# The low part of every second weight tile by a negated copy and an adding transfer

## The chip, the cores and the metric

The kernel runs on one core of a Trainium2 chip. The metric is the device time of one execution in microseconds. A profiled execution has besides its time a span, from its first to its last instruction, and every event in it is dated from the start of that span.

## The reference

A trunk of two layers works on 256 latent and 256 context tokens of width 1024. Each layer is a half-step SwiGLU feed-forward, a token mixer (chunked spatial gating beside a bidirectional gated linear recurrence, with one input and one output projection), and a second feed-forward. Cut to what matters here:

```python
def _swiglu(h, w1, w3, w2):
    return (jax.nn.silu(h @ w1) * (h @ w3)) @ w2
...
    for l in range(DEPTH):
        last = l == DEPTH - 1
        ml = _modulation(c, w_ada[l], b_ada[l])
        mc = _modulation(c_ctx[None], w_ada[l], b_ada[l])
        ...
        lat = lat + 0.5 * ml[2] * _swiglu(_modulate(lat, norm_ffn1_g[l], ml[0], ml[1]), *ffn1)
        cx = cx + 0.5 * mc[2] * _swiglu(_modulate(cx, norm_ffn1_g[l], mc[0], mc[1]), *ffn1)
        ...
        lat = lat + ml[5] * out_lat
        ...
        lat = lat + 0.5 * ml[8] * _swiglu(_modulate(lat, norm_ffn2_g[l], ml[6], ml[7]), *ffn2)
        if not last:
            cx = cx + 0.5 * mc[8] * _swiglu(_modulate(cx, norm_ffn2_g[l], mc[6], mc[7]), *ffn2)
    return _rmsnorm(lat, norm_final_g)
```

All weights are float32. In the last layer the context tokens are dropped after the mixer has read them, so the last feed-forward and most of the last mixer work on the 256 latent tokens alone. The modulation vectors (shift, scale, gate) come from `silu(c) @ w_ada`.

## The kernel before, in words

**Three products for one.** TensorE multiplies in the float32r format, which keeps fewer bits than float32. So every operand is held as a high part (the value rounded to float32r) and a low part (the value minus its high part), and `mm3` (L284 to L288) issues three matmuls for each product: high with high, high with low, low with high.

**Weight tiles.** The weights are cut into 362 tiles of up to 4 x 128 rows and 256 columns (512 KB; the last of each six in a down projection has 2 x 128 rows, 256 KB). `plan` (L102) lists them in the order in which they are used. A tile goes through three stages, and `pump` (L156) drives them:

- load: SyncE issues a transfer into a `wraw` buffer (L172 to L174). There are N_RAW = 3 of them, so the load of tile n+3 reuses the buffer of tile n and is issued right behind the split of tile n in the program.
- split: ScalarE writes the high part `whi` (L187, a copy with rounding), then VectorE writes the low part `wlo` (L191, source minus high part). There are N_SPLIT = 4 pairs of buffers, so the split of tile n waits until TensorE is done with tile n-4. `n_split` counts the splits and so numbers the tiles.
- use: `fm` (L290) and `tm_unit` (L680) run the matmuls of a tile; `done` (L209) counts it as finished.

`take` (L193) hands out the next tile and calls `pump` first, so that the split of tile i+3 is issued when tile i is taken. The same function `split` (L186) makes the parts of the gated activations (`g_hi`, `g_lo`) and of mixer activations (`h_hi`, `h_lo`).

**Modulation loads.** Between weight tiles the plan has 256 ada pieces. SyncE loads each (L166) into one of three `wada` buffers, on the same in-order queue as the weight loads; VectorE adds them up (`acc`, L247 and L249), TensorE turns the sum (`ada_ps`, L258), ScalarE copies it (L261).

**Order.** The schedule is manual: each engine runs its instructions in the order in which the program issues them, and semaphores hold them where data or buffers aren't ready. A feed-forward first runs 11 pairs of 256 hidden columns (two tiles of w1, two of w3 each: 44 tiles) and after each half the gate: silu on ScalarE (L422), the product on VectorE (L424), the split of the result. Then come four down projections of 256 columns, six tiles each. With both token groups a matmul has 512 moving columns; the last quarter of the down projection is done for latent and for context tokens apart (256 columns each, its six tiles loaded twice). In the last feed-forward all matmuls have 256 columns. Four PSUM banks take the products, two at a time.

**GpSimd** has little to do: the constants of the start, and the power in `rstd` (L331) for each norm, which VectorE's `spread` (L356) waits for. No transfer is issued on its queue.

Of the kernel before, what the change touches and what calls it, by code (L numbers as in the profile page):

```python
# [10 lines left out]
F32 = mybir.dt.float32  # L11
F32R = mybir.dt.float32r
U8 = mybir.dt.uint8
AF = mybir.ActivationFunctionType
ALU = mybir.AluOpType
# [57 lines left out]
class Trunk:  # L73
# [82 lines left out]
    def pump(self):  # L156
        nc = self.nc
        moved = True
        while moved:
            moved = False  # L160
            if self.n_load >= 4 and self.a_load < min(len(self.adas), self.a_done + self.N_ADA):
                it = self.adas[self.a_load]
                _, l, j, half, k = it.key
                c0 = j * D + 512 * half
                it.raw = self.wp.tile([P, 512], F32, tag="ada", name="wada", bufs=self.N_ADA)
                nc.sync.dma_start(it.raw, self.io["w_ada"][l, k * P:(k + 1) * P, c0:c0 + 512])  # L166
                self.a_load += 1
                moved = True
            if self.n_load < min(self.cap_load, len(self.ws), self.n_split + self.N_RAW):
                it = self.ws[self.n_load]  # L170
                _, name, l, k0, nk, c0 = it.key
                it.raw = self.wp.tile([P, 4, 256], F32, tag="raw", name="wraw", bufs=self.N_RAW)  # L172
                src = self.io[name][l, k0 * P:(k0 + nk) * P, c0:c0 + 256]
                nc.sync.dma_start(it.raw[:, :nk, :], src.rearrange("(k p) c -> p k c", p=P))  # L174
                self.n_load += 1
                moved = True
            if self.n_split < min(self.cap_split, self.n_load, self.n_done + self.N_SPLIT):
                it = self.ws[self.n_split]
                nk = it.key[4]
                it.hi = self.wp.tile([P, 4, 256], F32R, tag="hi", name="whi", bufs=self.N_SPLIT)  # L180
                it.lo = self.wp.tile([P, 4, 256], F32R, tag="lo", name="wlo", bufs=self.N_SPLIT)
                self.split(it.hi[:, :nk, :], it.lo[:, :nk, :], it.raw[:, :nk, :])
                self.n_split += 1
                moved = True

    def split(self, hi, lo, src):  # L186
        self.nc.scalar.activation(hi, src, AF.Copy)  # L187
        self.low(hi, lo, src)

    def low(self, hi, lo, src):  # L190
        self.nc.vector.tensor_tensor(lo, src, hi.bitcast(F32), op=ALU.subtract)  # L191
# [887 lines left out]
```

## Time and profile before

| what | value |
|---|---|
| time, median of two runs | 1818.21 us (1817.19 and 1819.23) |
| the profiled execution's own time | 1819.16 us |
| its span | 1817.5 us |
| granted TensorE clock, mean | 0.995 |
| bytes moved by transfers | 266.99 MB, 147 GB/s over the span |

In the profile an engine's busy time counts its instructions, not its waits. PE is TensorE's matmuls, PEld its weight loads, DVE VectorE, ACT ScalarE, POOL GpSimd, SP SyncE; a q behind a name means the engine's instruction queue, such as SPq for transfers issued by SyncE. A row of a group reads: line, engine, operation, written tile <- read tiles, shapes, count, then busy microseconds and mean nanoseconds of one, then the idle time just before them and what ended it. Rows of a timeline begin with the start and the duration in microseconds. Matmuls overlap, so the duration of one is longer than the distance between two.

### The profile page before, as it was taken

The page shows a single profiled execution, that of the slowest core. Times are in us where ns is not written, and L with a number is a line of the kernel's source. Part 1 is how long each engine was busy: PE and PEld are TensorE (multiplying, and loading weights), DVE is VectorE, ACT ScalarE, POOL GpSimd, SP SyncE. Part 2 cuts the span into 40 slices and gives each one's busy share as a digit, 9 for nine tenths or more (in the row PEclk, how much of TensorE's full clock was granted, in tenths as well). Part 3 has the DMA queues.
Part 4 walks back from the last instruction along what each step waited for, and adds up shares of the span by engine and source line. Part 5 has one row for each costly group of instructions (what it writes and reads, how often), then busy time and mean ns, then how long its engine had stood idle before and what let it go on. Part 6 is the DMA issues. An engine that isn't in the chain of part 4 may idle for free. (4 is left out here: it accounts for less than half of the span.)

```text
span 1817.5 us, 27049 instructions
## 1 busy us (share of the span) xinstructions
PE 1785.7 (98%) x10853; PEld 1547.7 (85%) x10853; DVE 1125.8 (62%) x1746; ACT 670.5 (37%) x1087; POOL 20.6 (1%) x27
## 2 busy tenths in 40 slices
PE   7999999999999999999999999999999999989998
PEld 5777778899898898777788897777788999979998
DVE  4766676675737666666666676545445767665554
ACT  3322222236444343222222242222222555544443
POOL 0000000000000000000000000000000000000000
PEclk9999999999999999999999999999999999989999
DMA  9555555554212124555454544544454532446653
GB/s 327 167 171 157 173 157 164 181 190 126 70 59 82 59 59 146 153 154 156 145 151 153 185 138 147 159 152 149 153 166 140 157 105 86 136 128 186 186 186 117
DMA packets 230645, 266.99 MB, mean 147 GB/s; under 512 B 10368, under 2 KB 192248, under 8 KB 230520
## 3 DMA queue, kind: packets, MB, share of 16 engines
q1 hardware_dynamic: 230520, 265.27, 47.2%
q8 instruction: 85, 1.39, 0.3%
q14 instruction: 40, 0.33, 0.1%
HBM read 264.18 MB, written 1.05 MB: 146 GB/s over the span
## 5 line engine op out<-in xcount | busy, mean ns | idle before, releaser
L286 PE MATMUL mm<-h_hi,whi 128*128 128x512 f32 (+1 forms) x2016 | 712.2, 353 | 4.9 <-ACT h_hi L383 3.0
L287 PE MATMUL mm<-h_lo,whi 128*128 128x512 f32 (+1 forms) x2016 | 705.2, 350 | 1.5 <-DVE h_lo L372 1.0
L288 PE MATMUL mm<-h_hi,wlo 128*128 128x512 f32 (+1 forms) x2016 | 702.6, 349 | 0.0
L191 DVE TENSOR_TENSOR wlo<-wraw,whi 128x1024 fp32r<-128x1024 f32 x362 | 430.7, 1195 | 371.8 <-ACT whi L187 367.8
L187 ACT ACTIVATE whi<-wraw 128x1024 fp32r<-128x1024 f32 x362 | 370.9, 1031 | 409.0 <-PE mm L287 288.0
L286 PEld LDWEIGHTS mm<-h_hi,whi 128*128 128x128 f32 x2016 | 381.0, 189 | 63.0 <-issue 4.0
L287 PEld LDWEIGHTS mm<-h_lo,whi 128*128 128x128 f32 x2016 | 382.7, 190 | 56.7 <-DVE h_lo L372 5.6
L288 PEld LDWEIGHTS mm<-h_hi,wlo 128*128 128x128 f32 x2016 | 380.7, 189 | 53.5
L286 PE MATMUL mm<-g_hi,whi 128*128 128x256 f32 (+1 forms) x836 | 282.1, 337 | 0.0
L288 PE MATMUL mm<-g_hi,wlo 128*128 128x256 f32 (+1 forms) x836 | 278.8, 334 | 0.0
L287 PE MATMUL mm<-g_lo,whi 128*128 128x256 f32 (+1 forms) x836 | 278.8, 333 | 0.0
L249 DVE SCALAR_TENSOR_TENSOR acc<-wada,cond,acc 128x512 f32<-128x512 f32 x392 | 274.0, 746 | 4.3 <-DMA wada<-in_w_ada_dram 3.4
L286 PEld LDWEIGHTS mm<-g_hi,whi 128*128 128x128 f32 x836 | 158.1, 189 | 18.3 <-issue 2.4
L288 PEld LDWEIGHTS mm<-g_hi,wlo 128*128 128x128 f32 x836 | 158.1, 189 | 16.0
L287 PEld LDWEIGHTS mm<-g_lo,whi 128*128 128x128 f32 x836 | 158.2, 189 | 15.2
L187 ACT ACTIVATE g_hi<-silu 128x512 fp32r<-128x512 f32 (+1 forms) x92 | 51.7, 562 | 182.9 <-DVE silu L424 181.0
L422 ACT ACTIVATE silu<-mm 128x512 f32<-128x512 f32 (+1 forms) x92 | 48.3, 528 | 139.7 <-PE mm L288 135.4
L191 DVE TENSOR_TENSOR g_lo<-silu,g_hi 128x512 fp32r<-128x512 f32 (+1 forms) x92 | 55.7, 605 | 57.9 <-ACT g_hi L187 57.9
L424 DVE TENSOR_TENSOR silu<-silu,mm 128x512 f32<-128x512 f32 (+1 forms) x92 | 54.9, 597 | 36.4 <-PE mm L288 36.4
L286 PE MATMUL mm<-whi,h_hi 128*128 128x256 f32 x224 | 64.3, 287 | 0.0
L287 PE MATMUL mm<-wlo,h_hi 128*128 128x256 f32 x224 | 62.6, 279 | 0.0
L288 PE MATMUL mm<-whi,h_lo 128*128 128x256 f32 x224 | 62.5, 279 | 0.0
(129 smaller groups left out, 1053.0 us busy)
## 6 DMA issues: line engine op xcount, KB each, us to landing
wraw<-in_ffn_w_dram SPq DMA_DIRECT2D x271, 512.0 KB, 4.3
wada<-in_w_ada_dram SPq DMA_DIRECT2D x256, 256.0 KB, 3.2
wraw<-in_w_in_dram SPq DMA_DIRECT2D x56, 512.0 KB, 3.6
a<-in_w_ada_dram SPq DMA_DIRECT2D x8, 1024.0 KB, 9.6
wraw<-in_w_out_dram SPq DMA_DIRECT2D x16, 512.0 KB, 3.9
wraw<-in_ffn_w_dram SPq DMA_DIRECT2D x19, 256.0 KB
x<-in_x_dram SPq DMA_DIRECT2D x2, 512.0 KB
ctx<-in_ctx_dram SPq DMA_DIRECT2D x2, 512.0 KB, 5.8
```

Source lines behind the costliest of these rows:

```text
L187: self.nc.scalar.activation(hi, src, AF.Copy)
L191: self.nc.vector.tensor_tensor(lo, src, hi.bitcast(F32), op=ALU.subtract)
L249: nc.vector.scalar_tensor_tensor(acc[:, s], raw, c, acc[:, s], op0=ALU.mult, op1=ALU.add)
L286: mm(ps, lhsT=l_hi, rhs=r_hi, start=start, stop=False)
L287: mm(ps, lhsT=l_hi, rhs=r_lo, start=False, stop=False)
L288: mm(ps, lhsT=l_lo, rhs=r_hi, start=False, stop=stop)
L422: nc.scalar.activation(silu[j], ps, AF.Silu)
L424: nc.vector.tensor_tensor(silu[j], silu[j], ps, op=ALU.mult)
```

## The change

In `pump`, the odd tiles from number 9 on take another way through the split. ScalarE writes the high part as before, then writes the negated high part (a copy of the source with scale -1 and the same rounding) into the low buffer. A transfer issued on GpSimd's queue then adds the source, from the raw buffer, onto the low buffer, which gives source minus high part. VectorE's subtraction falls away for these tiles. Activations are split as before.

```diff
                 it.lo = self.wp.tile([P, 4, 256], F32R, tag="lo", name="wlo", bufs=self.N_SPLIT)
-                self.split(it.hi[:, :nk, :], it.lo[:, :nk, :], it.raw[:, :nk, :])
+                parts = it.hi[:, :nk, :], it.lo[:, :nk, :], it.raw[:, :nk, :]
+                if self.n_split % 2 and self.n_split > 8:
+                    self.split_by_dma(*parts)
+                else:
+                    self.split(*parts)
                 self.n_split += 1
                 moved = True
...
+    def split_by_dma(self, hi, lo, src):
+
+        nc = self.nc
+        nc.scalar.activation(hi, src, AF.Copy)
+        nc.scalar.activation(lo, src, AF.Copy, scale=-1.0)
+        nc.gpsimd.dma_start(lo.bitcast(F32), src, accum_op=ALU.add)
```

## The prediction

> **What bounds the kernel now.** I read the page first: how full each engine is, and where over the span.
>
> ```profile
> span 1817.5 us, 27049 instructions
> PE 1785.7 (98%) x10853; PEld 1547.7 (85%) x10853; DVE 1125.8 (62%) x1746; ACT 670.5 (37%) x1087; POOL 20.6 (1%) x27
> PE   7999999999999999999999999999999999989998
> DMA  9555555554212124555454544544454532446653
> ```
>
> TensorE is busy for 1785.7 of 1817.5 us in nearly every slice, so all that could be won by feeding it better is 31.8 us, 1.7% of the span. VectorE at 62% and ScalarE at 37% are not the bound. The transfer engines are half busy, and they are busiest in the last eighth; I come back to that. Next the two rows of the split itself, and who waits for it.
>
> ```profile
> L191 DVE TENSOR_TENSOR wlo<-wraw,whi 128x1024 fp32r<-128x1024 f32 x362 | 430.7, 1195 | 371.8 <-ACT whi L187 367.8 <-PE aux L524 2.0 <-PE mm L287 1.3
> L187 ACT ACTIVATE whi<-wraw 128x1024 fp32r<-128x1024 f32 x362 | 370.9, 1031 | 409.0 <-PE mm L287 288.0 <-issue 109.8 <-DMA wraw<-in_ffn_w_dram 4.2
> ```
>
> ```profile
> SPq L174 <- DVE wlo L191: 931.3, 303, 17.1
> ```
>
> The split of a weight tile starts when TensorE gives a whi/wlo buffer back (the 288.0 us that ScalarE idles for L287). The second row, from the list of waits, is the one that matters: the loads on SyncE's queue wait 931.3 us, in 303 cases, for wlo, the subtraction that is the last reader of a raw buffer. Today that wait costs nothing, because a raw buffer comes free early. How early follows from the pace of the tiles, which I took from the timeline of ScalarE's splits, in the gated stage of layer 0 (512 columns, with ada loads between) and in the last feed-forward (256 columns).
>
> ```profile
> 783.72 1.05 ACT L187 ACTIVATE whi<-wraw 128x1024 fp32r<-128x1024 f32 x1
> ...
> 806.89 1.05 ACT L187 ACTIVATE whi<-wraw 128x1024 fp32r<-128x1024 f32 x1
> ```
>
> ```profile
> 1640.12 1.06 ACT L187 ACTIVATE whi<-wraw 128x1024 fp32r<-128x1024 f32 x1 [1.38 <-PE mm L287]
> 1644.37 1.05 ACT L187 ACTIVATE whi<-wraw 128x1024 fp32r<-128x1024 f32 x1
> ...
> 1651.51 1.06 ACT L187 ACTIVATE whi<-wraw 128x1024 fp32r<-128x1024 f32 x1 [1.46 <-PE mm L288]
> ```
>
> Three whi rows are left out inside the first fence, two inside the second: each fence spans four tiles, 23.2 us with 512 columns (5.8 us a tile) and 11.4 us with 256 (2.85 us a tile). In the last feed-forward everything is therefore wanted twice as fast. Its loads, from the window 1640 to 1680, and the engines in 45 us of it:
>
> ```profile
> L174 SPq DMA_DIRECT2D wraw<-in_ffn_w_dram x14: 367/368/368, 1640.0 to 1676.4; - x14
> DMA to landing us min/median/max: 3.7/3.8/4.0
> ```
>
> ```profile
> 1665.00:1710.00 45.00, 45.00 (x385) 45.00 (x383) 25.43 (x33) 22.51 (x32) 0.00 (x0) 1.00 0.64 186
> ```
>
> TensorE 45.00 of 45.00, transfers at a share of 0.64. In 45 us there are 45/2.85 = 15.8 tiles, so one 512 KB load holds all 16 transfer engines for 0.64 x 45/15.8 = 1.8 us; the other 2.0 us of its 3.8 are latency.
>
> **The change part by part.** The odd tiles from 9 to 361 change: 177 of 362.
>
> Removed: 177 subtractions, 177 x 1.195 = 211 us of VectorE. VectorE is not the bound, so this gives back only where a wlo stood on the chain that ended last. Those steps of a microsecond or more, outside the dense stages:
>
> ```profile
> 1401.17 1.23 DVE wlo L191
> ...
> 1436.71 2.27 DVE wlo L191 x2
> ...
> 1442.88 1.23 DVE wlo L191
> ...
> 1585.68 1.21 DVE wlo L191
> ...
> 1592.17 1.22 DVE wlo L191
> ...
> 1603.42 1.24 DVE wlo L191
> 1604.67 4.02 DMA wraw<-in_ffn_w_dram
> ...
> 1609.87 1.22 DVE wlo L191
> ```
>
> Together 9.6 us, half of them on odd tiles: at most 5 us, and since the replacement is not shorter I take 2.
>
> Added on ScalarE: 177 activations of the form of L187, 177 x 1.03 = 182 us, to 853 us, 47% of the span. In the window of 45 us above it goes from 22.5 by 8 x 1.06 to 31 us. It stays off the bound. Behind each on ScalarE stand the silu and g_hi of the gate, later by 1 us; the two spare PSUM banks cover that (a pair of tiles, 5.7 us). Without that cover it would be 1 us a gate.
>
> Added on GpSimd's queue: 177 transfers. Behind them in that queue stand only the powers of the norms.
>
> ```profile
> POOL r L331 <- DVE ms L329: 1771.6, 20, 367.3
> L331 POOL TENSOR_TENSOR r<-ms,mhalf 128x2 f32<-128x2 f32 (+3 forms) x20 | 19.0, 948 | 1771.6 <-DVE ms L329 1771.6
> ```
>
> Twenty of these, which VectorE's spread waits for; each may stand a microsecond or two behind a transfer whose negated part isn't written. I cost it at 1 us in all, as most norms run behind matmuls.
>
> Added wait, the one that counts: an odd tile's wlo, and the release of its raw buffer, come only when the adding transfer has landed. Call D the time from the end of the negation to that landing. No row of before shows such a transfer. Its bounds: it cannot well be shorter than the fastest plain load of such a tile, and with source read, destination read and result written one after another it would be three loads.
>
> ```profile
> DMA to landing us min/median/max: 3.3/4.1/10.7
> ```
>
> That row is for all loads of wraw over the span. So D lies between 3.3 us and 3 x 3.8 + 0.95 = 12.4 us (0.95 being GpSimd's own mean instruction, as its issue cost). The value: issue 0.95, two streams of reading 2 x 1.8 = 3.6, latency 2.0, and since loads will hold the same engines for 1.8 of every 4 us, some 1.5 us of waiting for them: D = 8.0 us, nearer to two loads than to one or to three.
>
> A rule of the Trainium skill gives a shorter D. In "DMA: Bandwidth & Descriptors", section "Anatomy of one DMA — SWDGE (gpsimd) path", a transfer from GpSimd's queue is put at 2.0 us plus its bytes at 436 GB/s; two reads of 512 KB would by that be an estimated 4.4 us, and the sum below would be an estimated +15 us instead of +97. The load rows above, 3.8 us where that formula says 3.2, speak for a little more. The same page, under "Issuing engines are not separate DMA queues", has all queues share the same 16 engines; by that the 1.5 us of waiting belongs in D, and no run here shows it yet.
>
> What follows for the tiles: let the split of odd tile n start at 0. Its two activations end at 2.1, the transfer lands at 2.1 + D. Only then may the load of tile n+3 go, into the same raw buffer (three of them), and the load of n+4 is behind it in SyncE's queue. The first lands 0.4 + 3.8 later, the second 1.8 after that, so the split of n+4, again an odd tile, starts no sooner than 2.1 + D + 6.0 = D + 8.1. That is the round for four tiles. It must be within 11.4 us at 256 columns (D up to 3.3) or 23.2 us at 512 (D up to 15.1). With D = 8.0 it is 16.1 us: free at 512 columns, and 16.1/4 = 4.03 us a tile at 256, 1.18 more than 2.85. The other round, of the whi/wlo buffer (2.1 + D + one tile of 2.85 = 13.0), is shorter and adds nothing.
>
> Where tiles go by at 256 columns:
>
> ```profile
> 1618.21 0.58 PE mm L287
> ...
> 1808.19 0.49 DVE x L397
> ```
>
> Between these rows, 190 us, lies the last feed-forward: 44 tiles up, 20 full and 4 half tiles down, worth 66. 66 x 1.18 = 78 us, less about 6 us for the tiles that are loaded and split ahead when it begins: 72. The tail of each of the other three feed-forwards has 12 such tiles (worth 11), 13 us; but a stretch of 512 columns leaves each split ready 3 x 5.8 - 2.1 - 8.0 = 7 us early, so 6 us each: 18. Layer 1's output projection, 8 tiles, 8 x 1.18 = 9. The rest of layer 1's mixer has the recurrence's matmuls between its tiles; I add nothing.
>
> Sum: 72 + 18 + 9 + 1 - 2 = +98. The profiled execution took 1819.2 us (span 1817.5, and 1.7 around it), 0.05% above the median of 1818.2 of the two runs. Rounded, the forecast is 1915 us.
>
> **The rivals.**
>
> First, not slower: the adding transfer is short. Place: the same raw-buffer round; point of decision: D of 3.3 us, where 11.4 us for four tiles still suffice. For it: source and destination both lie on the chip, and 3.3 us is seen for a load. Against it: it reads twice what a load reads, and a load takes 3.7 at its best in this stage. Then only VectorE's relief is left, 1819 - 2 = 1817 us; with D from 3.3 to 5 us, up to (13.1/4 - 2.85) x 66 + 7 = 35 us more. Faster than 1782 would need the whole idle time of TensorE.
>
> Second, the ada loads. They stand in SyncE's queue behind a weight load that now waits for D.
>
> ```profile
> 786.05 0.38 SPq L174 DMA_DIRECT2D wraw<-in_ffn_w_dram  x1
> 787.38 1.65 SPq L166 DMA_DIRECT2D wada<-in_w_ada_dram  x2
> ```
>
> ```profile
> wada<-in_w_ada_dram SPq DMA_DIRECT2D x256, 256.0 KB, 3.2
> ```
>
> ```profile
> 796.42 1.41 DVE L249 SCALAR_TENSOR_TENSOR acc<-wada,cond,acc 128x512 f32<-128x512 f32 x2
> ```
>
> ```profile
> L261 ACT ACTIVATE ada_sb<-ada_ps 128x128 f32<-128x128 f32 x36 | 9.9, 276 | 119.7 <-PE ada_ps L258 119.7
> ```
>
> The weight load would be 2.1 + 8.0 - 2.3 = 7.8 us late on an odd tile; the two ada loads behind it went out by 789, landed 3.2 later and were used at 796.4, 4 us to spare. VectorE's sums, and the ada_ps matmuls of TensorE (36 groups, 32 of them after the start), would then be up to 4 us late on half of the groups: 16 x 4 = 64 us, 1980 with the rest. Against it: TensorE reads the sums a whole tile later, 5.8 us. So this needs D over about 10.
>
> Third, D over 15.1 us, by slow issue on GpSimd or slow adding: the round exceeds 23.2 us and the 512-column stages slow too. At D = 18 the round is 26.1: (26.1/4 - 2.85) x 66 = 242, and some 230 tiles at 512 columns lose 0.7 each, 160: about 2220 us.
>
> **How the numbers follow.** Forecast (D from 5 to 10, slower, 1855 to 1960): 0.57, at 1915. Short transfer: 0.21, 1815 to 1855, of which 0.02 for a gain over 2% and 0.19 within 2%. Late ada loads with D from 10 to 15, 1960 to 2100: 0.14. Over 15: 0.08. The range 1836 to 2060 leaves out nearly half of the first rival, the top of the second and the third, 0.2 together. 2% is about what a measurement of this kernel can tell from no change. So faster 0.02, within 0.19, slower 0.79.
>
> **What would show it right or wrong.** Right: VectorE's wlo group at 185 instructions, ScalarE's copies of wraw at 539; a transfer wlo<-wraw on GpSimd's queue that lands about 8 us after its issue; the stages at 512 columns at 5.8 us a tile as now; the last feed-forward about 70 us longer, with four splits spanning some 16 us, ScalarE's whi waiting for wraw loads and SyncE's L174 waiting for the adding transfer instead of wlo. Wrong: a last feed-forward of 190 us (D was short), TensorE idle ahead of ada_ps (second rival), four tiles over 23.2 us in layer 0 (third), or TensorE waiting at tile starts with the raw loads in time, which would mean that wlo itself and not the raw buffer is late.

## The result and the profile after

The changed kernel takes 1923.7 us (median of two runs, 1921.2 and 1926.1) against 1818.2: a ratio of 1.058 with a 95% interval from 1.056 to 1.061, so 105 us slower. The profiled execution took 1921.2 us with a span of 1919.5. Its line numbers have moved by some ten from L191 on: the subtraction is L202 now, the matmuls are L297 to L299, and the new way through the split is L197 (high part), L198 (negated high part) and L199 (the transfer).

The top of the page after:

```profile
span 1919.5 us, 27434 instructions
PE 1805.5 (94%) x10853; PEld 1561.4 (81%) x10853; DVE 932.2 (49%) x1569; ACT 827.7 (43%) x1264; POOL 174.4 (9%) x204
PE   7999999989999989999999899999998998778887
PEclk9999999999999999999999899999999999899999
DMA  9677777785343338677677767767668546688886
```

VectorE is freed by 194 us and nothing comes of it. TensorE's idle time went from 31.8 to 114.0 us (1919.5 - 1805.5), and its busy time rose by 19.8 us for the same matmuls. The slices show where: the middle is as full as before but for a single eight here and there; the last six are not. By the cut points of the stages (windows of both traces, each ending, to within a tile or two, where the split of the same tile starts):

| stretch | before, us | after, us | more |
|---|---|---|---|
| start and first feed-forward, up to its tail | 380 | 380.5 | 0.5 |
| its tail, first tiles of the mixer | 52 | 62.5 | 10.5 |
| rest of layer 0's mixer | 208 | 208 | 0 |
| end of its output projection, next feed-forward's first tiles | 60 | 67 | 7 |
| second feed-forward, 512 columns | 310 | 310 | 0 |
| its tail, first tiles of layer 1 | 82 | 97 | 15 |
| layer 1's first feed-forward, 512 columns | 298 | 298 | 0 |
| its tail, first tiles of the mixer | 68 | 76 | 8 |
| layer 1's mixer and output projection, up to the last norm | 162 | 172 | 10 |
| last feed-forward | 188 | 239 | 51 |
| end | 9.5 | 9.5 | 0 |

Two rows of those windows for the last feed-forward, of before and then of after. Columns: window, length, busy time of PE, PEld, DVE, ACT and POOL, granted clock, share of the transfer engines, GB/s.

```profile
1620.00:1744.00 124.00, 124.00 (x1045) 123.93 (x1045) 71.63 (x92) 62.50 (x89) 0.00 (x0) 0.99 0.61 181
1744.00:1808.00 64.00, 64.00 (x535) 63.94 (x533) 30.02 (x38) 23.06 (x30) 0.00 (x0) 1.00 0.45 144
```

```profile
1671.00:1832.00 161.00, 130.76 (x1052) 127.39 (x1052) 45.14 (x72) 83.12 (x113) 18.95 (x22) 0.96 0.82 204
1832.00:1910.00 78.00, 66.92 (x534) 65.50 (x532) 20.05 (x28) 32.37 (x42) 9.46 (x11) 0.98 0.77 194
```

ScalarE works 83 of 161 us there, so it isn't the bound. The transfers' share has risen from 0.61 and 0.45 in the two parts (0.56 over the stage) to 0.82 and 0.77 (0.80). The groups of the page that name the new wait, and the queues (packets, MB, share of 16 engines; q1 is SyncE's, q0 GpSimd's) with the issue row:

```profile
L299 PE MATMUL mm<-h_hi,wlo 128*128 128x512 f32 (+1 forms) x2016 | 708.4, 351 | 53.5 <-DMA wlo<-wraw 53.5
...
L199 POOL DMA_DIRECT2D wlo<-wraw x177 | 153.7, 868 | 1611.8 <-ACT wlo L198 1451.4
```

```profile
q1 hardware_dynamic: 230520, 265.27, 43.3%
q0 software_dynamic: 25488, 87.83, 24.6%
...
wlo<-wraw POOLq DMA_DIRECT2D x158, 512.0 KB, 5.2
```

One adding transfer costs GpSimd 0.87 us and lands 5.2 us after its issue. Of all 16 engines it takes 0.246 x 1919.5 / 167.5 = 2.8 us (158 of 512 KB and 19 of half the size count as 167.5); a load of 512 KB takes 0.433 x 1919.5 / 506 = 1.64 us (265.27 MB are 506 such loads). And the waits, total, times and longest:

```profile
ACT whi L191 <- DMA wraw<-in_ffn_w_dram: 77.2, 38, 5.2
...
PE mm L299 <- DMA wlo<-wraw: 75.4, 33, 5.4
...
PE ada_ps L269 <- DVE acc L260: 0.6, 2, 0.3
```

```profile
SPq L174 <- DMA wlo<-wraw: 1019.1, 174, 18.6
SPq L174 <- DVE wlo L202: 195.3, 58, 14.0
```

SyncE's loads wait for the adding transfer where they waited for VectorE. But now someone waits for the loads (ScalarE, 77.2 us at the copies of the even tiles), and TensorE waits for the low part itself (75.4 us), where its product with the low part (L288) waited for nothing before. The ada loads do come later: VectorE waits 84.6 us for them, against 3.4 before. But TensorE still waits only 0.6 us for their sums, as before, so the rival of the late ada loads is out. In the last feed-forward the chain of work that ended last no longer runs through TensorE. The fence shows one round from its middle, and the first and the last step of ten rounds (start, duration, what; "issue" covers the two activations and GpSimd's start):

```profile
1676.88 4.95 DMA wlo<-wraw
...
1749.41 5.14 DMA wlo<-wraw
1754.56 6.80 DMA wraw<-in_ffn_w_dram
1761.43 2.33 issue
1763.77 6.05 DMA wlo<-wraw
...
1823.81 5.93 DMA wlo<-wraw
```

Adding transfer, load, two activations, adding transfer. From 1676.88 to 1823.81 there are ten rounds of four tiles: 14.7 us each, 3.67 us a tile, where TensorE needs 2.85.

### The profile page after: what moved, and what is told of

Read it like the earlier page. It is cut to its first block, busy times and chain, and to the rows that moved or that the text cites. A ratio compares the mean times of both kernels' runs of the same rounds, so it can differ in the third digit from the quotient of the medians.

```text
span 1919.5 us, 27434 instructions
## 1 busy us (share of the span) xinstructions
PE 1805.5 (94%) x10853; PEld 1561.4 (81%) x10853; DVE 932.2 (49%) x1569; ACT 827.7 (43%) x1264; POOL 174.4 (9%) x204
## 3 DMA queue, kind: packets, MB, share of 16 engines
q1 hardware_dynamic: 230520, 265.27, 43.3%
## 4 chain that ended last, share of the span: by engine, by line
PE 74%; DMA 15%; issue 4%; ACT 3%; DVE 3%; SPq 0%; POOL 0%; ACTq 0%; POOLq 0%; DVEq 0%
PE mm L297 23%; PE mm L299 23%; PE mm L298 23%; DMA wlo<-wraw 8%; DMA wraw<-in_ffn_w_dram 6%; PE aux L535 2%; PE ada_ps L269 1%; ACT wlo L198 1%; ACT whi L191 1%; DVE wlo L202 1%; DMA wraw<-in_w_in_dram 1%; DVE tmp L393 1%; ACT whi L197 1%; PE o L615 1%; DMA a<-in_w_ada_dram 1%
## 5 line engine op out<-in xcount | busy, mean ns | idle before, releaser
L299 PE MATMUL mm<-h_hi,wlo 128*128 128x512 f32 (+1 forms) x2016 | 708.4, 351 | 53.5 <-DMA wlo<-wraw 53.5
L297 PE MATMUL mm<-h_hi,whi 128*128 128x512 f32 (+1 forms) x2016 | 715.3, 355 | 3.2 <-ACT h_hi L394 3.0
L299 PEld LDWEIGHTS mm<-h_hi,wlo 128*128 128x128 f32 x2016 | 385.8, 191 | 112.1 <-DMA wlo<-wraw 58.5
L202 DVE TENSOR_TENSOR wlo<-wraw,whi 128x1024 fp32r<-128x1024 f32 x185 | 226.4, 1224 | 437.2 <-ACT whi L191 420.3
L297 PEld LDWEIGHTS mm<-h_hi,whi 128*128 128x128 f32 x2016 | 386.3, 192 | 60.9 <-issue 4.0
L191 ACT ACTIVATE whi<-wraw 128x1024 fp32r<-128x1024 f32 x185 | 195.3, 1057 | 297.5 <-PE mm L298 155.0
L260 DVE SCALAR_TENSOR_TENSOR acc<-wada,cond,acc 128x512 f32<-128x512 f32 x392 | 275.2, 747 | 85.6 <-DMA wada<-in_w_ada_dram 84.6
L299 PE MATMUL mm<-g_hi,wlo 128*128 128x256 f32 (+1 forms) x836 | 281.8, 337 | 22.0 <-DMA wlo<-wraw 22.0
L199 POOL DMA_DIRECT2D wlo<-wraw x177 | 153.7, 868 | 1611.8 <-ACT wlo L198 1451.4
L297 PE MATMUL mm<-g_hi,whi 128*128 128x256 f32 (+1 forms) x836 | 284.2, 340 | 0.0
L197 ACT ACTIVATE whi<-wraw 128x1024 fp32r<-128x1024 f32 (+1 forms) x177 | 178.0, 1005 | 114.5 <-PE mm L298 55.7
L299 PEld LDWEIGHTS mm<-g_hi,wlo 128*128 128x128 f32 x836 | 160.8, 192 | 39.6 <-DMA wlo<-wraw 23.8
L198 ACT ACTIVATE wlo<-wraw 128x1024 fp32r<-128x1024 f32 (+1 forms) x177 | 176.8, 999 | 0.0
L297 PEld LDWEIGHTS mm<-g_hi,whi 128*128 128x128 f32 x836 | 160.8, 192 | 18.5 <-issue 2.2
L191 ACT ACTIVATE g_hi<-silu 128x512 fp32r<-128x512 f32 (+1 forms) x92 | 51.7, 562 | 183.0 <-DVE silu L435 183.0
L202 DVE TENSOR_TENSOR g_lo<-silu,g_hi 128x512 fp32r<-128x512 f32 (+1 forms) x92 | 55.7, 606 | 57.9 <-ACT g_hi L191 57.9
```

Source lines behind the costliest of these rows:

```text
L198: nc.scalar.activation(lo, src, AF.Copy, scale=-1.0)
L199: nc.gpsimd.dma_start(lo.bitcast(F32), src, accum_op=ALU.add)
L260: nc.vector.scalar_tensor_tensor(acc[:, s], raw, c, acc[:, s], op0=ALU.mult, op1=ALU.add)
L297: mm(ps, lhsT=l_hi, rhs=r_hi, start=start, stop=False)
L299: mm(ps, lhsT=l_lo, rhs=r_hi, start=False, stop=stop)
```

## The experiments

My theory after the result was the forecast's: the raw buffer comes back late, so the loads are late. Its rivals: the low part itself lands too late for TensorE (only four whi/wlo pairs), or the transfer engines are too full. The changed kernel shows signs of all three. First I checked where the loss lies; then I took the two waits apart in the last feed-forward.

**The last feed-forward alone.**

```diff
-                if self.n_split % 2 and self.n_split > 8:
+                if self.n_split % 2 and self.n_split >= 294:
```

> The change for the odd tiles of the last feed-forward alone (34 of 177). In the changed kernel that stage took 239 us where it took 188 before. If the loss arises where tiles go by at 256 columns, and no earlier stage's delay carries into it, this run alone shows 50 us of the 105: about 1868 us, with the earlier stages as before. If half of the loss came from the earlier transfers (a queue that fills up, a clock that stays lower), it shows less than 40.

Measured: 1871.3 us, one run, against a median of 1815.5 for the kernel before on that chip: 56 us. The stage alone costs at least what it costs in the whole change (51 us in the table), so no delay of an earlier stage is needed to explain it.

**The long stretches at 512 columns alone.**

```diff
-                if self.n_split % 2 and self.n_split > 8:
+                if self.n_split % 2 and any(a <= self.n_split < b for a, b in ((9, 60), (79, 105), (119, 173), (193, 249))):
```

> The change for the odd tiles of the long stretches at 512 columns alone (94 of 177: 9 to 59, 79 to 103, 119 to 171, 193 to 247). All theories that put the loss at the narrow stages expect 1818 us within 4, half of all transfers for nothing, and no gain from VectorE's 112 us either. A theory by which each added transfer costs something (sharing of the transfer engines, a slower ScalarE) expects 94/177 of 105, so about 1874.

Measured: 1815.5 us against 1815.5, ratio 1.0001 (0.9991 to 1.0012). At 512 columns 94 added transfers cost nothing that these runs can tell from zero. The window 700 to 1000 of this kernel, and then of the kernel before:

```profile
700.00:1000.00 300.00, 300.00 (x1422) 241.01 (x1422) 162.23 (x239) 108.57 (x138) 21.68 (x26) 1.00 0.69 196
```

```profile
700.00:1000.00 300.00, 300.00 (x1426) 240.47 (x1424) 189.16 (x264) 83.34 (x108) 0.00 (x0) 1.00 0.52 155
```

27 us less of VectorE, 25 us more of ScalarE, a share of 0.69 for the transfers, and TensorE full in both: no time won, none lost.

**Only the raw buffer late.** The negated copy goes into a buffer of its own, the transfer adds the source onto that, and VectorE makes the low part.

```diff
-        nc.scalar.activation(lo, src, AF.Copy, scale=-1.0)
-        nc.gpsimd.dma_start(lo.bitcast(F32), src, accum_op=ALU.add)
+        neg = self.gp.tile([P, 4, 256], F32, tag="neg", name="neg", bufs=2)[:, :hi.shape[1], :]
+        nc.scalar.activation(neg, src, AF.Copy, scale=-1.0)
+        nc.gpsimd.dma_start(neg, src, accum_op=ALU.add)
+        self.low(hi, lo, src)
```

> Last feed-forward alone. ScalarE writes the negated copy into a buffer of its own and the transfer adds the source onto that, unused; VectorE makes the low part as before. So the raw buffer is given back as late as in the change, and the low part is early. Raw-buffer theory: 40 to 50 us lost, as in the change of this stage alone. Low-part theory (TensorE waits because the low part itself lands late, four whi/wlo buffers): 0 to 5 us. Theory of shared transfer engines: at most (6.1/2 - 2.85) x 66 = 13 us, two loads of 1.64 us and one adding transfer of 2.82 us of all 16 engines in every two tiles.

Measured: 1859.7 us, one run: 44 us.

**Only the low part late.** The split is the one of before; then a transfer adds zeros onto the low part.

```diff
-        nc.scalar.activation(hi, src, AF.Copy)
-        nc.scalar.activation(lo, src, AF.Copy, scale=-1.0)
-        nc.gpsimd.dma_start(lo.bitcast(F32), src, accum_op=ALU.add)
+        self.split(hi, lo, src)
+        nc.gpsimd.dma_start(lo.bitcast(F32), self.zero[:, :hi.shape[1], :], accum_op=ALU.add)
```

> Last feed-forward alone. The split as before, and then a transfer adds a buffer of zeros onto the low part of the odd tiles. So the raw buffer is given back as early as before, and the low part lands as late as in the change (1.05 + 1.2 + some 6 us after the start of the split). Raw-buffer theory: 0 to 5 us lost. Low-part theory: 40 to 50 us. Theory of shared transfer engines: some 13 us.

Measured: 1859.6 us, one run: 44 us too. So the theory that only the raw buffer counts has fallen, and so has each theory of a single wait: either wait alone gives much of the loss. The waits in the window 1620 to 1800 show that the two kernels did what they were made for, first the late raw buffer, then the late low part:

```profile
ACT whi L192 <- DMA wraw<-in_ffn_w_dram: 44.5, 20, 4.4
```

```profile
PE mm L299 <- DMA wlo<-zero: 27.8, 19, 3.1
...
ACT whi L192 <- DMA wraw<-in_ffn_w_dram: 3.6, 2, 2.1
```

With the raw buffer free early, the loads no longer hold back, and the adding transfers take longer. Two steps, one round apart, of the chain of the second kernel:

```profile
1709.74 7.05 DMA wlo<-zero
...
1723.27 7.04 DMA wlo<-zero
```

13.5 us a round, with landings of 7.0 instead of some 5.5 us in the chain of the whole change. So this kernel makes the low part later than the change does, and its 44 us may overstate what the change's own low part costs; the run with five raw buffers below has the change's own transfer. The longer landing pointed at the transfer engines, and at opening the rounds one by one.

**Beside it, with nobody waiting.** As the kernel with only the raw buffer late, but the transfer reads zeros, so neither the raw buffer nor the low part waits for it.

```diff
-        nc.gpsimd.dma_start(neg, src, accum_op=ALU.add)
+        nc.gpsimd.dma_start(neg, self.zero[:, :hi.shape[1], :], accum_op=ALU.add)
```

> Last feed-forward alone. The split as before; besides it ScalarE writes a negated copy into a buffer of its own and the transfer adds zeros onto that: as many bytes moved and as many instructions as in the change, but neither the raw buffer nor the low part waits for the transfer. If the two waits are the whole cause: 0 to 5 us lost. If the transfer engines are full (share 0.88 to 0.93 in the three runs of this stage; 0.93 x 60 us over some 17.6 tiles is 3.17 us a tile against 2.85): 13 to 21 us, with a share near 1.

Measured: 1833.3 us, one run beside 1814.9 for the kernel before: 18 us lost with no wait for the transfer at all. A window, the queues in it, and ScalarE's wait for loads from 1620 to 1800:

```profile
1680.00:1740.00 60.00, 57.23 (x487) 55.75 (x486) 31.64 (x41) 35.79 (x50) 8.71 (x10) 1.00 1.02 265
```

```profile
q1 hardware_dynamic: 10672, 10.60, 57.1%
q0 software_dynamic: 1440, 5.24, 44.2%
...
wraw<-in_ffn_w_dram SPq DMA_DIRECT2D x20, 512.0 KB, 7.4
```

```profile
ACT whi L192 <- DMA wraw<-in_ffn_w_dram: 23.5, 16, 2.9
```

The engines' share is 1.02, a load lands after 7.4 us instead of 3.8, and with three raw buffers ScalarE waits for loads again. Twenty loads and ten adding transfers in 60 us: 1.71 and 2.65 us of all engines for one, 6.1 us for two tiles, by this count 3.04 a tile against TensorE's 2.85. Whether that count is a floor, the last of the next three kernels tells.

**More buffers.** The change in the last feed-forward alone, with two more raw buffers, two more whi/wlo pairs, or both, from that stage's own pool (the limits in `pump` rise with them; those lines are left out).

```diff
+                if self.gp and self.n_load % 5 > 2:
+                    it.raw = self.gp.tile([P, 4, 256], F32, tag="raw", name="wraw", bufs=2)
...
+                pool, bufs = (self.gp, 2) if self.gp and self.n_split % 6 > 3 else (self.wp, 4)
```

> The change in the last feed-forward alone, with five raw buffers instead of three there. Raw buffer alone to blame: 0 to 5 us lost instead of 55. Two rounds one behind the other (the raw buffer's, and that of the four whi/wlo buffers): the second shows now, as in the run in which only the low part was late, some 44 us.

> The change in the last feed-forward alone, with six whi/wlo buffer pairs instead of four there and three raw buffers. Low part alone to blame: 0 to 5 us lost. Two rounds: the raw buffer's stays, some 44 us.

> The change in the last feed-forward alone, with five raw buffers and six whi/wlo pairs there. If waits of a latency are all there is, both rounds are opened and 0 to 5 us are lost. If the transfer engines are the floor beneath them: 13 to 21 us lost at a share near 1.

Measured, one run each beside 1814.9: five raw buffers 1853.4 (39 us lost), six pairs 1874.4 (60 us, more than was expected and no gain at all), both 1828.4 (13.5 us). The waits of the first in the window 1620 to 1800, then of the second:

```profile
PE mm L303 <- DMA wlo<-wraw: 22.3, 12, 6.0
...
ACT whi L195 <- DMA wraw<-in_ffn_w_dram: 2.9, 4, 0.9
```

```profile
ACT whi L193 <- DMA wraw<-in_ffn_w_dram: 40.9, 19, 4.2
...
PE mm L299 <- DVE silu L439: 19.2, 10, 2.7
...
PE mm L301 <- DMA wlo<-wraw: 2.6, 4, 0.9
```

In the change of this stage alone, in the same window, ScalarE's wait for loads is 42.1 us and TensorE's for the low part 26.3. So each pool removes its own wait, and the other stays about as it was. With six pairs TensorE waits for the gate's product instead (19.2 us), probably because ScalarE, in whose order the gate's silu stands behind a split, is still waiting for a load; that was not tested. Only both pools together bring TensorE near its old pace. Two windows of the kernel with both, and then the same windows of the kernel before:

```profile
1620.00:1660.00 40.00, 33.20 (x249) 32.34 (x249) 12.89 (x21) 23.60 (x33) 5.21 (x6) 0.88 0.86 219
1660.00:1780.00 120.00, 119.89 (x1030) 119.69 (x1030) 40.58 (x60) 73.25 (x100) 18.05 (x21) 1.00 1.04 273
```

```profile
1620.00:1660.00 40.00, 40.00 (x332) 39.93 (x332) 24.48 (x34) 20.71 (x30) 0.00 (x0) 0.97 0.55 160
1660.00:1780.00 120.00, 120.00 (x1015) 120.00 (x1015) 65.78 (x82) 57.28 (x79) 0.00 (x0) 1.00 0.62 186
```

What is left, 13.5 us, has the size that was expected of a floor set by the bytes, (6.1/2 - 2.85) x 66 = 13, but the agreement proves nothing, for it isn't lost where such a floor would act. From 1660 to 1780 TensorE is full and runs as many matmuls as before, while the transfer engines stand at 1.04. Most of it is lost at the start of the stage, from 1620 to 1660: 83 matmuls fewer in the records, 6.8 us idle and a clock of 0.88. One adding transfer in the chain there takes 9.23 us; what else makes the start slow was not taken apart.

So the loss of the last feed-forward is two latency rounds, of the raw buffers and of the whi/wlo pairs. The engines that both queues share lengthen every landing in them; that they hold TensorE down by themselves, once both pools are large enough, is not shown, and this window speaks against it.

**The narrow places between.** The forecast had 18 us for three tails and nothing for the tiles that are kept through two passes. The first diff is the tails, the second the kept tiles.

```diff
+                if self.n_split % 2 and any(a <= self.n_split < b for a, b in ((61, 74), (171, 184), (245, 258))):
```

> The change for the odd tiles of the three tails alone (last quarter of a down projection, twelve tiles at 256 columns, and the tile before: 21 of 177). The forecast had 6 us for each, 18 in all, and nothing for what follows a tail. The delays of the changed kernel's splits, tile by tile, rise by some 12 us over these tiles. So 12 to 18 us over the kernel before.

```diff
+                if self.n_split % 2 and any(a <= self.n_split < b for a, b in ((74, 79), (105, 119), (184, 193), (258, 267))):
```

> The change for the odd tiles alone that are kept through a pass over the latent and one over the context tokens, or come just behind such tiles (17 of 177; the first four of layer 0's and layer 1's mixer, the end of layer 0's output projection with the first of the second feed-forward, the first of layer 1's first feed-forward). The forecast had nothing for them: in the two passes a tile takes 5.7 us. If what is lost there follows from the tails ahead, 0 to 4 us. If the four buffer pairs are what counts (all are held during the first pass, and the next splits start one by one in the second), some 20 to 28 us, as the delays of the changed kernel's splits rise by 28 over these tiles.

Measured beside 1816.9 for the kernel before: tails 1833.6 us, ratio 1.0097 (1.0080 to 1.0114), by that ratio 18 us; kept tiles 1838.8, ratio 1.0128 (1.0109 to 1.0147), 23 us. The waits of the first, then of the second, over the whole run:

```profile
ACT whi L191 <- DMA wraw<-in_ffn_w_dram: 16.8, 7, 6.1
PEld mm L299 <- DMA wlo<-wraw: 11.5, 4, 5.7
```

```profile
PEld mm L299 <- DMA wlo<-wraw: 18.5, 7, 4.9
...
ACT whi L191 <- DMA wraw<-in_ffn_w_dram: 3.5, 3, 2.1
```

In the tails both are late; at the kept tiles it is the low part, with no more waiting for loads than before the change (3.5 us against 4.2). The kept tiles' loss is their own and no echo of the tails. Stretches at 512 columns 0, tails 18, kept tiles 23, last feed-forward 56: 97 of the 105 us. The rest fits layer 1's mixer and output projection (10 us more in the table), whose 14 changed tiles from 267 to 293 were not run alone. No version came out faster than the kernel before; the best equals it.

## Why the prediction was right, and where it was off

The time (1915 forecast, 1923.7 measured) and the main place were right: nothing at 512 columns, the loss where tiles go by at 256. So was the round of the raw buffer. The size of single terms was not, and the errors made up for each other: 21 us too much for the last feed-forward, 23 us too little for the kept tiles. That the sum came within 9 us is in part luck.

- **VectorE's relief, ScalarE's extra copies.** Forecast 2 us won, nothing lost. Right: VectorE's share fell and the wide stretches stayed as they were to 0.1%.
- **D, 8.0 us.** Too long. From issue to landing it was 5.2 us over the span and 5.9 in the last feed-forward, and some 0.3 us lie ahead of the issue. The Trainium skill's formula ("DMA: Bandwidth & Descriptors", section "Anatomy of one DMA — SWDGE (gpsimd) path"), with two reads an estimated 4.4 us, was too short for these landings. I counted 3.6 us of all engines for the two reads; the trace has 2.8. The landings of all adding transfers from 1671 to 1910:

```profile
DMA to landing us min/median/max: 3.5/5.9/7.3
```

- **The round of four tiles, 16.1 us.** Measured 14.7. The chain is the one that was forecast: transfer, load, two activations. With D at 5.9 + 0.3 my own formula, D + 8.1, would have given 14.3; the loads in the chain took 6.5 us in the mean of ten (6.80 in the round shown) and not 6.0.
- **The last feed-forward, +72 us.** Measured +51, or 56 with the change there alone: (3.67 - 2.85) x 66 - 6 = 48 by the measured round. The term was mis-sized by D.
- **The other round, of the whi/wlo pairs, "adds nothing".** This is the step that failed. I had worked out 13.0 us for it and didn't note that this too is above 11.4. In the last feed-forward it lay just beneath the first round, so my sum there didn't suffer; but the run with five raw buffers still lost 39 us to it, and at the kept tiles it was the wait that counted. The last of my signs of being wrong, TensorE waiting for wlo itself, was seen too: 75.4 us, though beside late loads and not in place of them.
- **Tails 18 us, kept tiles without a term.** Measured 18 and 23. The prediction doesn't name the kept tiles; the reason for that, 5.7 us a tile in two passes, stands only in the text written ahead of their own run. That is a mean pace, and TensorE waited there for the low part. Which tiles of such a place are to blame was not taken apart further.
- **Layer 1's output projection, 9 us.** The stretch that holds it took 10 us longer; it was not run alone, so this term is neither confirmed nor refuted.
- **The transfer engines.** I used their share only to stretch D. My loads went by 3.8 us from issue to landing; beside adding transfers for which nobody waits it was 7.4, and that kernel lost 18 us in the last feed-forward.
- **The rivals.** The ada loads came later, but TensorE waited 0.6 us for their sums as before. A D above 15 and one below 3.3 are both out.
- **The sums.** The terms add up to 98; the 97 named beside the skill's estimate is the rounded forecast of 1915 less 1818. ScalarE came to 827.7 us and not 853. That 2% is about the least that a measurement can tell was too cautious: the runs of this kernel tell 0.1 to 0.2%.

One cost was in no term: the clock. The granted clock's mean is 0.982 after and 0.995 before, 0.96 in the window of the last feed-forward, and TensorE's busy time rose by 19.8 us for the same 10853 matmuls. By the Trainium skill ("TensorE: Matmul & The Clock Gate", Part 1, on the HAM clock gate) the clock is halved after an idle window of about 3.4 us. The longest waits here, 5.4 us, would be enough for that, but the trace also has a lower clock behind a wait of 2.1 us, with none longer since 1711, and there the measurement decides. The end of that wait, and the windows around it, in the last feed-forward of after:

```profile
1724.83 0.38 PE L299 MATMUL mm<-h_hi,wlo 128*128 128x256 f32 x1 [2.08 <-DMA wlo<-wraw]
```

```profile
1721.00:1724.00 3.00, 1.75 (x16) 1.55 (x14) 1.23 (x1) 2.89 (x5) 0.00 (x0) 1.00 1.06 236
1724.00:1727.00 3.00, 2.17 (x13) 2.17 (x14) 0.00 (x0) 0.61 (x1) 0.86 (x1) 0.78 0.69 193
1727.00:1731.00 4.00, 4.00 (x29) 4.00 (x28) 2.13 (x4) 1.47 (x2) 0.00 (x0) 0.74 0.99 225
```

What a wait must be like to lower the clock stays open, and no run took the clock's cost apart from the waits themselves.

## What to carry to other kernels

An engine's relief is worth something only where that engine ends a wait; here 194 us of VectorE bought nothing, since TensorE was at 98%. Here the transfer lengthened the time for which every buffer it touches is held. So work out the round of each buffer pool at the pace of the fastest stage, and compare each of them with that pace, not only the longest: enlarging one pool won 17 us or nothing, enlarging both won 42 of 56. Ask also what the added bytes do to the landing of the other queue's loads. And look apart at places where several tiles are held at once; a mean pace hid 23 us there.

## What the runs showed of the hardware

Transfers from GpSimd's queue and from SyncE's share the same 16 engines: with nobody waiting for the adding transfers the share reached 1.02, and the landing of a 512 KB load went from 3.8 to 7.4 us. The Trainium skill says so ("DMA: Bandwidth & Descriptors", section "Issuing engines are not separate DMA queues"), and the trace agrees. The share that the profile shows is no measure of what is left: at 1.04 over 120 us TensorE still got all its tiles in time, with both pools larger. An adding transfer of 512 KB within the on-chip memory took 2.65 to 2.8 us of all 16 engines, 1.5 to 1.7 times a load of that size, and 0.87 us of GpSimd to issue.
